# Latent attention with two 64-row tiles in the TensorE array

## The chip, the cores and the metric

The kernel runs on one core of a Trainium2 chip. A core has TensorE (matrix products, into PSUM), VectorE, ScalarE and GpSimd (element by element), and SyncE, whose queue here issues nearly all transfers. A matmul holds a stationary operand of up to 128 rows and 128 columns, loaded ahead of it, and streams a moving operand of up to 512 columns through it. The metric is the device time of one execution in microseconds; less is better. The time of the kernel before is the median of three runs.

## The reference

Two layers over 1024 latent tokens and 256 context tokens, width 1024: a windowed attention, then a multi-head latent attention; at the end a normalisation. The change is in the second layer's attention. It has 16 heads. Queries and keys have 64 dimensions without position ("nope") and 32 with rotary position ("rope"); the rope keys are shared by all heads. Only latent tokens are queries, 1280 tokens are keys:

```python
q  = (rms_norm(cq, q_norm) @ w_uq).reshape(b, n, 16, 64 + 32)
kv = (rms_norm(ckv, kv_norm) @ w_ukv).reshape(b, n, 16, 64 + 64)
# kn, v: halves of kv; kr: one 32-wide rope key for all heads
s = (einsum("bqhd,bkhd->bhqk", qn, kn) + einsum("bqhd,bkd->bhqk", qr, kr)) * scale
p = softmax(s, axis=-1)
o = einsum("bhqk,bkhd->bqhd", p, v)
y = (o * silu(g)) @ w_out
```

## The kernel before

All products but a few are made in three matmuls of reduced-precision float32 operands: each operand is split into a high part and a remainder, and high x high, remainder x high and high x remainder are summed in PSUM (`mm3`, lines 125 to 127). `split` (lines 120 and 121) makes the parts: ScalarE casts, VectorE or GpSimd subtracts.

The latent attention runs over 32 units, one per head and half of the queries (512). Keys of a head lie as 100 rows by 1280 columns in one of three buffers: 64 nope rows, 32 rope rows and four rows of ones. Queries lie the same way, and their last four rows take the negative row maxima, so that the product already holds score minus maximum. A unit has these steps:

- `prep`: two loads from DRAM bring its queries.
- `top(b)`, for four blocks of 128 queries: three matmuls (line 1122; 512, 512 and 256 keys, high parts only) write the scores into PSUM banks 0 to 2, and VectorE reduces them to the negative maximum (line 1126).
- `shift`: TensorE transposes the maxima (line 1130), ScalarE writes them into the query rows in four pieces (line 1133).
- `score(c)`, for ten key blocks of 128: `mm3` into one of banks 3 to 5, ScalarE takes the exponential (line 1141), GpSimd adds it to a running sum (lines 1145 and 1148), for the denominators.
- `PV`: ten plain float32 matmuls (line 1156), each run by the chip as two, of 64 stationary columns; even key blocks go to output rows 0 to 63, odd ones to 64 to 127. `fin` adds the two halves (lines 1170, ScalarE, and 1171, VectorE).
- `fin2`: four transpositions (line 1181) of the running sum and a VectorE sum (line 1182). `fin3`, for every second head only, brings the reciprocals to the rows by four more (line 1199), multiplies (line 1200, then GpSimd) and stores.

Every fourth unit makes the next two heads' keys (`make_K`, three blocks, each 6 matmuls, split into the key buffers), and every eighth the values of four heads (`make_V`, 60 matmuls of 256 columns). The third product matrix `w_out` is loaded and split in 16 pieces meanwhile, and when the last unit runs, the output tiles (`out_tiles`) begin.

A loop at the end interleaves the steps: between the ten scores of a unit stand the maxima of the next, `fin2` and `fin3` of the one before and pieces of K, V and `w_out`. The tile framework then sets the order of each engine's instructions from its own priorities, so that a matmul can move ahead of one that stands before it in the source; each engine then runs its list strictly in order, and semaphores make it wait for operands and for buffers.

## Time and profile before

| | |
|---|---|
| median of 3 runs | 1681.49 us (1681.13 to 1683.01) |
| profiled execution, span | 1678.9 us |
| TensorE busy | 1594.1 us, 95% |
| VectorE, ScalarE, GpSimd busy | 996.2, 831.6, 808.4 us |
| first value product starts | 1060.0 us |
| value products 9 and 17 start | 1199.1 and 1335.6 us |
| matmuls of the maxima (line 1122) | 384 |
| reductions of the maxima (line 1126) | 128, 1488 ns each |
| exponentials (line 1141) | 320, 597 ns each |

Rows of the trace in order of time give the start, the duration (merged for neighbours of one kind, with their count behind the x), the engine, the line, the operation, the output and input, their shapes and, in brackets, how long the engine was idle before it and what ended that. PE is TensorE's matmuls, PEld its weight loads, DVE VectorE, ACT ScalarE, POOL GpSimd, SPq the queue on SyncE. A matmul's duration runs to its result and so overlaps with its successor; what a matmul costs is read from start to start. In the rows by stretch stand the stretch, its length, busy time and count of PE, PEld, DVE, ACT and POOL, the granted clock, the transfer share and GB/s.

### The profile page before, as it was taken

The page shows a single profiled execution, that of the slowest core. Times are in us where ns is not written, and L with a number is a line of the kernel's source. Part 1 is how long each engine was busy: PE and PEld are TensorE (multiplying, and loading weights), DVE is VectorE, ACT ScalarE, POOL GpSimd, SP SyncE. Part 2 cuts the span into 40 slices and gives each one's busy share as a digit, 9 for nine tenths or more (in the row PEclk, how much of TensorE's full clock was granted, in tenths as well). Part 3 has the DMA queues.
Part 4 walks back from the last instruction along what each step waited for, and adds up shares of the span by engine and source line. Part 5 has one row for each costly group of instructions (what it writes and reads, how often), then busy time and mean ns, then how long its engine had stood idle before and what let it go on. Part 6 is the DMA issues. An engine that isn't in the chain of part 4 may idle for free.

```text
span 1678.9 us, 24936 instructions
## 1 busy us (share of the span) xinstructions
PE 1594.1 (95%) x8724; PEld 1247.4 (74%) x8724; DVE 996.2 (59%) x2004; ACT 831.6 (50%) x1790; POOL 808.4 (48%) x780
## 2 busy tenths in 40 slices
...
PEclk9999869999999999999999999999999999999999
...
GB/s 309 139 170 164 149 176 163 50 151 161 119 104 101 95 89 89 89 53 229 39 49 229 231 89 58 110 50 24 61 32 32 54 20 54 33 88 70 46 157 63
DMA packets 134206, 175.78 MB, mean 105 GB/s; under 512 B 11184, under 2 KB 79408, under 8 KB 134080
## 3 DMA queue, kind: packets, MB, share of 16 engines
...
HBM read 127.99 MB, written 46.15 MB: 104 GB/s over the span
## 4 chain that ended last, share of the span: by engine, by line
PE 72%; DVE 11%; ACT 6%; issue 5%; POOL 4%; DMA 2%; SPq 0%; DVEq 0%; POOLq 0%; ACTq 0%
PE PB L125 15%; PE PB L127 15%; PE PB L126 15%; PE PB L1156 9%; PE PB L1122 4%; PE PB L583 3%; PE PB L573 3%; DVE arena_r L121 2%; DVE arena_f L194 2%; PE PB L545 2%; DVE arena_f L552 1%; POOL arena_f L446 1%; PE PB L546 1%; DMA arena_f<-ada_w 1%; DVE arena_f L275 1%
## 5 line engine op out<-in xcount | busy, mean ns | idle before, releaser
L125 PE MATMUL PB<-arena_r 128*128 128x512 f32 (+3 forms) x1816 | 639.5, 353 | 20.3 <-DVE arena_f L445 13.4
L126 PE MATMUL PB<-arena_r 128*128 128x512 f32 (+3 forms) x1816 | 630.7, 348 | 3.6 <-DVE arena_r L280 2.6
L127 PE MATMUL PB<-arena_r 128*128 128x512 f32 (+3 forms) x1816 | 627.8, 347 | 0.6 <-DVE arena_r L121 0.6
L125 PEld LDWEIGHTS PB<-arena_r 128*128 128x128 f32 (+1 forms) x1816 | 346.2, 191 | 97.3 <-issue 26.0
L127 PEld LDWEIGHTS PB<-arena_r 128*128 128x128 f32 (+1 forms) x1816 | 345.5, 191 | 42.5 <-DVE arena_r L121 1.2
L126 PEld LDWEIGHTS PB<-arena_r 128*128 128x128 f32 (+1 forms) x1816 | 346.7, 191 | 40.5 <-DVE arena_r L280 4.5
L1148 POOL TENSOR_TENSOR arena_f<-arena_f 128x512 f32<-128x512 f32 x252 | 326.0, 1294 | 76.9 <-ACT arena_f L1141 61.9
L1141 ACT ACTIVATE arena_f<-PB 128x512 f32<-128x512 f32 x320 | 188.8, 597 | 124.5 <-PE PB L127 110.5
L1126 DVE TENSOR_REDUCE arena_f<-PB 128x1 f32<-128x1280 f32 x128 | 190.4, 1488 | 96.5 <-PE PB L1122 94.1
L121 DVE TENSOR_TENSOR arena_r<-PB,arena_r 128x512 fp32r<-128x512 f32 (+4 forms) x255 | 162.5, 644 | 139.7 <-ACT arena_r L120 138.2
L121 POOL TENSOR_TENSOR arena_r<-arena_f,arena_r 128x512 fp32r<-128x512 f32 x98 | 139.4, 1437 | 182.9 <-ACT arena_r L120 139.8
L120 ACT CAST arena_r<-PB 128x512 fp32r<-128x512 f32 (+4 forms) x255 | 137.8, 549 | 68.7 <-PE PB L573 29.7
L552 DVE CUSTOM_DVE_ANT_0 arena_f<-PB,arena_f,small 128x256 f32<-128x256 f32 (+1 forms) x288 | 145.7, 523 | 28.0 <-PE PB L546 21.8
L1156 PE MATMUL PB<-arena_f 128*64 128x512 f32 x640 | 156.0, 599 | 0.0
L194 DVE SCALAR_TENSOR_TENSOR arena_f<-arena_f,small 128x512 f32<-128x512 f32 x126 | 125.8, 1042 | 22.2 <-DMA arena_f<-ada_w 22.0
L555 ACT ACTIVATE arena_f<-arena_f,small 128x640 f32<-128x640 f32 (+2 forms) x160 | 119.4, 747 | 28.4 <-DVE small L554 27.1
L120 ACT CAST arena_r<-arena_f 128x512 fp32r<-128x512 f32 (+2 forms) x146 | 86.7, 609 | 86.6 <-DVE arena_f L455 18.6
L583 PE MATMUL PB<-arena_r 128*128 128x512 f32 x336 | 123.2, 440 | 4.4 <-ACT arena_f L594 3.2
L573 PE MATMUL PB<-ident,arena_f 128*128 128x128 f32 x672 | 110.5, 274 | 1.1 <-ACT arena_f L555 1.0
L1156 PEld LDWEIGHTS PB<-arena_f 128*64 128x64 f32 x640 | 43.4, 136 | 80.4 <-issue 79.2
L1122 PE MATMUL PB<-arena_r 96*128 96x512 f32 (+1 forms) x384 | 100.3, 369 | 1.0 <-DVE arena_f L1126 0.9
L573 PEld LDWEIGHTS PB<-ident,arena_f 128*128 128x128 f32 x672 | 83.4, 140 | 19.4 <-ACT arena_f L555 5.0
...
## 6 DMA issues: line engine op xcount, KB each, us to landing
arena_f<-ada_w SPq DMA_DIRECT2D x82, 256.0 KB, 3.3
arena_r<-q_d SPq DMA_DIRECT2D x80, 256.0 KB, 4.0
arena_f<-a_w_in SPq DMA_DIRECT2D x40, 256.0 KB, 3.0
...
g_d<-arena_f SPq DMA_DIRECT2D x36, 256.0 KB, 3.2
...
arena_r<-qn_d SPq DMA_DIRECT2D x32, 256.0 KB, 3.5
```

The source lines that it names most:

```text
L120: nc.scalar.copy(hi, src)
L121: (lo_eng or nc.vector).tensor_sub(lo, src, hi.bitcast(F32))
L125: nc.tensor.matmul(o, ah, bh, start=first, stop=False)
L126: nc.tensor.matmul(o, al, bh, start=False, stop=False)
L127: nc.tensor.matmul(o, ah, bl, start=False, stop=last)
L573: nc.tensor.transpose(pt[:, h, :], self.Ps[h][:, ci * 128 : ci * 128 + 128], ident)
L583: nc.tensor.matmul(self.pv, V[:, self.chunks[ci], self.g, :], PT[:, s], start=ci == 0 and s == 0, stop=ci == self.m - 1 and s == 1,)
L1122: nc.tensor.matmul(psm[:, n0 : n0 + n], self.qT[0:96, 0, b * 128 : b * 128 + 128], kt[0:96, 0, n0 : n0 + n], start=True, stop=True,)
L1126: nc.vector.reduce_max(self.mx[:, 96 + b : 97 + b], psm[:, 0:TOK], AX.X, negate=True)
L1141: nc.scalar.activation(E, S, AF.Exp)
L1148: eng.tensor_add(self.acc, self.acc, E)
L1156: nc.tensor.matmul(self.pv[p : p + 64], Vq[:, c, self.h % 4, :], self.E.pop(c), start=c < 2, stop=c >= NT - 2)
```

## The change

Scores and maxima are taken with 64 stationary rows instead of 100. The upper and the lower 64 rows of the array form two tiles; matmuls on them use different rows and write different PSUM banks.

- **Keys.** A head's nope keys lie twice 64 rows by 768 columns: rows 0 to 63 hold key blocks 0 to 3, rows 64 to 127 blocks 4 to 7, and both hold blocks 8 and 9. There are four such buffers. The rope keys, the same for all heads, are made once: `kr1` has high part and remainder in 64 rows, `kr2` the high part and four rows of ones.
- **Queries.** They lie on both tiles, so `prep` issues eight loads instead of two. `shift` writes the maxima by two VectorE multiplies instead of four ScalarE ones.
- **Scores.** Key blocks go in pairs, one on each tile, in five passes (three for nope, two for rope): ten matmuls instead of six for two blocks. One exponential takes 1024 columns.
- **Maxima.** Two matmuls of 512 keys on each tile and two of 256 on one of them, six instead of three.
- **PSUM.** Scores, shift, `fin2`, `fin3`, K and V share two slots of two banks (banks 3 to 6) in turn; the value product has bank 7.
- **Order.** The value product of a unit stands behind the first two scores of the next, with `fin`, the shift, `fin3` and `fin2` behind it. TensorE runs in source order from the first unit on; the other engines' orders are still made by the framework.
- **w_out** is staged in one buffer instead of three.

On TensorE, around the value product of a unit without K or `fin3`, before (a row of L125 to L127 is a score's matmul, L1122 a maximum, L1130 the shift's transposition, L1156 the value product):

```order
L125 MATMUL PB<-arena_r 128x512
L1130 MATMUL PB<-ident,arena_f 100x128
L126 MATMUL PB<-arena_r 128x512
L127 MATMUL PB<-arena_r 128x512
L1122 MATMUL PB<-arena_r 128x512 x2
L1122 MATMUL PB<-arena_r 128x256
L1156 MATMUL PB<-arena_f 64x512 x10
L125 MATMUL PB<-arena_r 128x512
```

And now (L1144 and L1147 are a maximum, L1175 scores, L1197 the value product, L1154 the shift, L1222 `fin2`):

```order
L1175 MATMUL PB<-arena_r 128x512 x16
L1144 MATMUL PB<-arena_r 128x512 x4
L1147 MATMUL PB<-arena_r 128x256 x2
L1197 MATMUL PB<-arena_f 64x512 x10
L1154 MATMUL PB<-ident,arena_f 100x128
L1222 MATMUL PB<-ident,arena_f 128x128 x4
L1144 MATMUL PB<-arena_r 128x512 x4
L1147 MATMUL PB<-arena_r 128x256 x2
L1175 MATMUL PB<-arena_r 128x512 x16
```

The shift's transposition has moved from ahead of the value product to behind it, `fin2` from the middle of the scores to the same place.

On VectorE at the same place, before (L1171 `fin`'s add, L1126 a maximum, L1182 `fin2`'s sum):

```order
L1171 TENSOR_TENSOR arena_f<-PB,arena_f 64x512
L1126 TENSOR_REDUCE arena_f<-PB 128x1
L1182 TENSOR_REDUCE small<-PB 128x4
L1126 TENSOR_REDUCE arena_f<-PB 128x1 x3
L1171 TENSOR_TENSOR arena_f<-PB,arena_f 64x512
```

And now (L1156 the shift's multiplies, L1212 `fin`'s add, L1223 `fin2`'s sum, L1149 a maximum, L1151 the copy of the maxima):

```order
L1149 TENSOR_REDUCE arena_f<-PB 128x1 x3
L1151 COPY arena_f<-arena_f 128x4
L1156 TENSOR_TENSOR arena_r<-PB,ident 4x512
L1212 TENSOR_TENSOR arena_f<-PB,arena_f 64x512
L1156 TENSOR_TENSOR arena_r<-PB,ident 4x512
L1223 TENSOR_REDUCE small<-PB 128x4
L1149 TENSOR_REDUCE arena_f<-PB 128x1 x4
```

Four instructions now stand between the fourth maximum of one unit and the first of the next; before, one stood between two maxima.

On TensorE where K is made, now, with the semaphores that an instruction waits for (L1237 is `fin3`, L125 to L127 K's product):

```order
L1197 MATMUL PB<-arena_f 64x512 x10
L1154 MATMUL PB<-ident,arena_f 100x128 [waits DVE_49,Activation_49]
L1237 MATMUL PB<-ident,arena_f 128x128 [waits Activation_49]
L1237 MATMUL PB<-ident,arena_f 128x128 x3
L1222 MATMUL PB<-ident,arena_f 128x128 [waits Pool_49]
L1222 MATMUL PB<-ident,arena_f 128x128 x3
L125 MATMUL PB<-arena_r 128x512 [waits DVE_49]
```

K's first matmul now waits for VectorE, which has to be done with the slot's last user.

The diff, cut:

```diff
--- before
+++ after
...
+    PAIRS = ((0, 4), (1, 5), (2, 6), (3, 7), (8, 9))
...
-    kTb = [r_at(o, 2, TOK) for o in (0, 16, 26)]
-    qtr = Ring(R, [10, 36, 40], 1024)
-    Er = Ring(F, [10 + 2 * c for c in range(NT)], 512)
-    accr = Ring(F, [30, 32], 512)
+    kTb = [r_at(6 * i, 2, 768) for i in range(4)]
+    kr1, kr2 = r_at(24, 768), r_at(27, 768)
+    qtb = [[r_at(o, 2, 512), r_at(o1, 512), r_at(o2, 512)] for o, o1, o2 in ((30, 34, 36), (38, 42, 112), (104, 108, 110))]
+    qt0 = [[r_at(o, 2, 512), r_at(o + 4, 512), r_at(o + 6, 512)] for o in (80, 88)]
+    Er = Ring(F, [10 + 4 * i for i in range(6)], 1024)
...
+    psm = PB[:, 0:3, :]
+    slots = Banks((3, 2), (5, 2))
+    pv_bank = PB[:, 7, :]
...
+    def slot():
+        return shp(slots(), 2, 512)
...
+    def make_kr():
...
+            w = slice(512 * (n // 2), 512 * (n // 2) + 128 * cn)
+            for t in (0, 1) if n == 2 else (n,):
+                p = 64 * t
+                src = pt[0:32, 0 : cn * 128]
+                split(kr1[p : p + 32, w], kr1[p + 32 : p + 64, w], src)
+                nc.scalar.copy(kr2[p : p + 32, w], src)
+        for p in (32, 96):
+            nc.gpsimd.tensor_copy(kr2[p : p + 4], const[p : p + 4, 0:1].to_broadcast([4, 768]))
...
+    def make_K(pair, blocks):
+        sl = slot()
+        for j, blk in enumerate(blocks):
+            n0, n = ((0, 512), (512, 512), (1024, 256))[blk]
+            ps = sl[:, j]
...
+        for j, blk in enumerate(blocks):
+            w = slice(0, 512) if blk < 2 else slice(512, 768)
             for e in range(2):
-                kt = kTb[(2 * pair + e) % 3]
-                split(kt[0:64, 0, n0 : n0 + n], kt[0:64, 1, n0 : n0 + n], ps[64 * e : 64 * e + 64, 0:n])
...
+                kt = kTb[(2 * pair + e) % 4]
+                for t in (0, 1) if blk == 2 else (blk,):
+                    p = 64 * t
+                    split(kt[p : p + 64, 0, w], kt[p : p + 64, 1, w], sl[64 * e : 64 * e + 64, j, 0 : w.stop - w.start])
...
         def prep(self):
-            q = shp(qtr.next(), 2, 512)
+            self.q = n, r1, r2 = qt0[self.i] if self.i < 2 else qtb[self.i % 3]
             ts = slice(self.half * 512, self.half * 512 + 512)
             e, r = 64 * self.e, 32 * (self.h % 4)
-            load(out=q[0:64].bitcast(F32), in_=qn_d[self.pair, e : e + 64, :, ts])
-            load(out=q[64:96].bitcast(F32), in_=qr_d[self.h // 4, r : r + 32, :, ts])
-            self.qT = q
+            for t in range(2):
+                load(out=n[64 * t : 64 * t + 64].bitcast(F32), in_=qn_d[self.pair, e : e + 64, :, ts])
+            for t in range(4):
+                load(out=r1[32 * t : 32 * t + 32].bitcast(F32), in_=qr_d[self.h // 4, r : r + 32, 0, ts])
+            for t in range(2):
+                load(out=r2[64 * t : 64 * t + 32].bitcast(F32), in_=qr_d[self.h // 4, r : r + 32, 1, ts])
             self.mx = mxr.next()
 
         def top(self, b):
-            kt = kTb[self.h % 3]
-            for n0, n in KEYB:
-                nc.tensor.matmul(
-                    psm[:, n0 : n0 + n], self.qT[0:96, 0, b * 128 : b * 128 + 128], kt[0:96, 0, n0 : n0 + n],
-                    start=True, stop=True,
+            n, r1, _ = self.q
+            bs = slice(b * 128, b * 128 + 128)
+            pairs = ((n[:, 0, bs], self.kt[:, 0]), (r1[:, bs], kr1))
+            rs = [slice(64 * t, 64 * t + 64) for t in range(2)]
+            for i, (q, k) in enumerate(pairs):
+                for t in range(2):
+                    nc.tensor.matmul(psm[:, t], q[rs[t]], k[rs[t], 0:512], start=i == 0, stop=i == 1)
+            for i, (q, k) in enumerate(pairs):
+                r = rs[b % 2]
+                nc.tensor.matmul(psm[:, 2, 0:256], q[r], k[r, 512:768], start=i == 0, stop=i == 1)
+            flat = psm.rearrange("p a b -> p (a b)")[:, 0:TOK]
+            nc.vector.reduce_max(self.mx[:, 32 + b : 33 + b], flat, AX.X, negate=True)
+            if b == 3:
+                nc.vector.tensor_copy(self.mx[:, 96:100], self.mx[:, 32:36])
+
+        def shift(self, pm):
+            nc.tensor.transpose(pm[0:100, 0:128], self.mx[:, 0:100], ident)
+            for p in (32, 96):
+                nc.vector.tensor_mul(
+                    shp(self.q[2][p : p + 4], 4, 128),
+                    pm[p : p + 4, 0:128].unsqueeze(1).to_broadcast([4, 4, 128]),
+                    ident[p : p + 4, p : p + 4].unsqueeze(2).to_broadcast([4, 4, 128]),
                 )
-            nc.vector.reduce_max(self.mx[:, 96 + b : 97 + b], psm[:, 0:TOK], AX.X, negate=True)
-
-        def shift(self):
-            pm = psx()[:, 0:128]
-            nc.tensor.transpose(pm[0:100], self.mx[:, 0:100], ident)
-            for b in range(4):
-                o = self.qT[96:100, 0, b * 128 : b * 128 + 128]
-                nc.scalar.activation(o, pm[96:100], AF.Copy, scale=ident[96:100, 96 + b : 97 + b])
-
-        def score(self, c):
-            kt = kTb[self.h % 3]
-            S = pst4()
-            cs = slice(c * 128, c * 128 + 128)
-            mm3(S, [kt[0:100, s, cs] for s in range(2)], [self.qT[0:100, s] for s in range(2)], True, True)
-            E = Er.next()
-            nc.scalar.activation(E, S, AF.Exp)
-            self.E[c] = E
-            if c == 1:
+
+        def score(self, i, a=0, b=5, hold=False):
+            n, r1, r2 = self.q
+            kt = self.kt
+            if a == 0:
+                self.S = slot()
+            S = self.S
+            c0 = (i * 128, i * 128) if i < 4 else (512, 640)
+            passes = [(kt[:, 0], n[:, 0], 64), (kt[:, 1], n[:, 0], 64), (kt[:, 0], n[:, 1], 64)]
+            passes += [(kr1, r1, 64), (kr2, r2, 36)]
+            for j in range(a, b):
+                k, q, rows = passes[j]
+                for t in range(2):
+                    r = slice(64 * t, 64 * t + rows)
+                    nc.tensor.matmul(S[:, t], k[r, c0[t] : c0[t] + 128], q[r], start=j == 0, stop=j == 4)
+            if b == 5 and not hold:
+                self.expo(i)
+
+        def expo(self, i):
+            E = shp(Er.next(), 2, 512)
+            nc.scalar.activation(E, self.S, AF.Exp)
+            self.E[i] = E
+            if i == 0:
                 self.acc = accr.next()
-                nc.gpsimd.tensor_add(self.acc, self.E[0], E)
-            elif c:
-                eng = nc.vector if self.i == NU - 1 and c > 5 else nc.gpsimd
-                eng.tensor_add(self.acc, self.acc, E)
+                nc.gpsimd.tensor_add(self.acc, E[:, 0], E[:, 1])
+                return
+            for t in range(2):
+                eng = nc.vector if self.i == NU - 1 and i > 2 else nc.gpsimd
+                eng.tensor_add(self.acc, self.acc, E[:, t])
 
         def PV(self):
-
-
-            self.pv = psv()
-            for c in range(NT):
-                p = 64 * (c % 2)
-                nc.tensor.matmul(
-                    self.pv[p : p + 64], Vq[:, c, self.h % 4, :], self.E.pop(c), start=c < 2, stop=c >= NT - 2
-                )
+            self.pv = pv_bank
+            for i, cs in enumerate(PAIRS):
+                E = self.E.pop(i)
+                for t in range(2):
+                    p = 64 * t
+                    nc.tensor.matmul(
+                        self.pv[p : p + 64], Vq[:, cs[t], self.h % 4, :], E[:, t], start=i == 0, stop=i == 4
+                    )
...
+        st = f_at(45, 512)
+        pieces = [(k, slice(c * 512, c * 512 + 512)) for k in (0, 1, 2, 3, 4, 6, 7, 5) for c in range(2)]
+        for i in range(len(pieces) + 1):
+            if i:
+                k, cs = pieces[i - 1]
+                split(WoB[k][:, 0, cs], WoB[k][:, 1, cs], st)
...
                 k, cs = pieces[i]
-                st = ring.next()
                 load(out=st, in_=t["b_w_out"][k * 128 : k * 128 + 128, cs])
...
-                yield
+            yield
...
+    with tc.manual_schedule(engines={mybir.EngineType.PE}):
+        u1.top(0)
+        u0.shift(slot()[:, 0])
+        u1.top(1)
+        for ui, u in enumerate(units):
+            pu, ppu = [units[ui - n] if ui >= n else None for n in (1, 2)]
+            nu, nnu = [units[ui + n] if ui + n < NU else None for n in (1, 2)]
+            if nnu:
                 nnu.prep()
-            u.score(c)
-            if nnu and c == 9:
+            u.score(0, 0, 2)
+            if nu:
+                nu.top(2)
+            u.score(0, 2, 5)
+            u.score(1, hold=True)
+            if nu:
+                nu.top(3)
+            if ui % 2 and 5 <= ui < 24 or 25 <= ui:
+                next(wo_fill, None)
+            if ui == NU - 1:
+                next(wo_fill, None)
+                next(out_fill)
+            if pu:
+                pu.PV()
+                u.expo(1)
+                pu.fin()
+                sl = slot()
+                if nu:
+                    nu.shift(sl[:, 0])
+                if ppu and ppu.e == 1:
+                    ppu.fin3(slot()[:, 0])
+                pu.fin2(sl[:, 1])
+            else:
+                u.expo(1)
+                nu.shift(slot()[:, 0])
+            if ui % 4 == 0 and u.pair < 7:
+                make_K(u.pair + 1, (0, 2))
+            if ui % 4 == 1 and u.pair < 7:
+                make_K(u.pair + 1, (1,))
+            if ui and ui % 8 == 0:
+                for _ in make_V(u.pair // 2):
+                    pass
+            if ui == NU - 1:
+                next(out_fill)
+            if nnu:
                 nnu.top(0)
-            if c == 9:
...
+            u.score(2)
+            u.score(3, 0, 3)
+            if nnu:
+                nnu.top(1)
+            u.score(3, 3, 5)
+            u.score(4)
...
```

`hold` keeps the exponential of the second score back until the value product stands in the lists; `fin`, `fin2` and `fin3` take the slot that they are handed and are otherwise as before.

156 lines of the change are left out of this document (49 added, 107 removed).

## The prediction

> **What bounds the kernel now.** I read the page's engine totals first, then the busy time of stretches cut at the starts of value products eight units apart.
>
> ```profile
> PE 1594.1 (95%) x8724; PEld 1247.4 (74%) x8724; DVE 996.2 (59%) x2004; ACT 831.6 (50%) x1790; POOL 808.4 (48%) x780
> PEclk9999869999999999999999999999999999999999
> 1199.10:1335.60 136.50, 136.17 (x651) 88.87 (x650) 69.18 (x69) 73.14 (x147) 97.42 (x76) 1.00 0.13 41
> 1335.60:1472.00 136.40, 136.07 (x649) 88.87 (x648) 69.50 (x69) 72.75 (x147) 97.05 (x76) 1.00 0.12 39
> ```
>
> In the latent-attention stage TensorE sets the time: eight units take 136.5 us, TensorE is busy for 136.2 of them at full clock (1.00), and VectorE (69) and ScalarE (73) have half their time free. One unit costs 136.5 / 8 = 17.06 us. The order of time on TensorE shows what that consists of:
>
> ```profile
> 1199.13 4.51 PE L1156 MATMUL PB<-arena_f 128*64 128x512 f32 x20
> 1203.57 0.50 PE L125 MATMUL PB<-arena_r 100*128 100x512 f32 x1
> 1203.91 0.39 PE L126 MATMUL PB<-arena_r 100*128 100x512 f32 x1
> 1204.13 0.40 PE L127 MATMUL PB<-arena_r 100*128 100x512 f32 x1
> 1204.37 0.75 PE L1122 MATMUL PB<-arena_r 96*128 96x512 f32 x3
> 1204.95 0.39 PE L125 MATMUL PB<-arena_r 100*128 100x512 f32 x1
> 1207.03 0.60 PE L1181 MATMUL PB<-ident,arena_f 128*128 128x128 f32 x4
> 1207.39 0.84 PE L1122 MATMUL PB<-arena_r 96*128 96x512 f32 x3
> 1208.06 0.39 PE L125 MATMUL PB<-arena_r 100*128 100x512 f32 x1
> ...
> 1212.93 0.75 PE L1122 MATMUL PB<-arena_r 96*128 96x512 f32 x3
> 1213.61 4.51 PE L1156 MATMUL PB<-arena_f 128*64 128x512 f32 x20
> ```
>
> Durations overlap, so I count from start to start. A score matmul steps 0.23 (1203.91 to 1204.13). A maximum (three matmuls of 512, 512, 256 keys) takes 0.58 (1204.37 to 1204.95), so 0.23 + 0.23 + 0.12. The value product takes 4.44 to the next matmul (1199.13 to 1203.57), and that one's successor comes 0.34 later, not 0.23. Four transpositions take 1208.06 - 1207.03 - 0.58 = 0.45. A unit without extras is 30 x 0.23 + 4 x 0.58 + 4.44 + 0.45 + about 0.3 = 14.4. Eight of them, two K products (each 12 steps of 0.23 and 6 of 0.12: 3.5), one V product (60 x 0.12 = 7.2) and four `fin3` (0.45 each) make 131; so about 5 us in 136.5 are waits.
>
> **What the change removes and adds on TensorE.** Scores: 25 pairs of matmuls instead of 30 matmuls. The price of a pair is not in the trace. The nearest rows are weight loads of the value product, whose two 64-column halves already lie side by side:
>
> ```profile
> 1214.09 0.14 PEld L1156 LDWEIGHTS PB<-arena_f 128*64 128x64 f32 x2 [0.29 <-issue]
> 1214.52 0.14 PEld L1156 LDWEIGHTS PB<-arena_f 128*64 128x64 f32 x2 [0.28 <-issue]
> 1204.84 0.19 PEld L125 LDWEIGHTS PB<-arena_r 100*128 100x128 f32 x1
> 1204.96 0.19 PEld L126 LDWEIGHTS PB<-arena_r 100*128 100x128 f32 x1
> ```
>
> Two loads share one 0.14, and twenty matmuls fit into 10 steps of 0.43 (4.3 of the 4.44): the halves run at the same time. Bounds for a pair: 0.23 (wholly side by side), 0.38 (two loads of 0.19 in series), 0.46 (two matmuls in series). I take 0.235: the value product is the nearest row, and two 128-column loads were started 0.12 apart, so even serial loads nearly fit. Scores: 25 x 0.235 = 5.9 instead of 6.9, a gain of 1.0. A maximum becomes two pairs and two matmuls of 256 on one tile, 2 x 0.235 + 2 x 0.12 = 0.71; four of them 2.84 instead of 2.32, a loss of 0.5. The switch into the value product's column tiles costs 0.1 (1212.93 to 1213.61 is 0.68, not 0.58), the way out another 0.1 (4.44 against 4.3) and 0.11 for the weight load behind it (0.34 against 0.23). A unit now has three modes (rows, columns, whole array) instead of two: 0.2 more. A plain unit's matmuls come to 14.1, 0.3 less than now. So TensorE has little to win; without any wait a mean unit would be 14.1 + 0.22 (`fin3`) + 0.87 (K) + 0.9 (V) = 16.1.
>
> **The waits that come in.** TensorE is now in source order, with nothing of another unit to slip in. The rows that price what it waits for:
>
> ```profile
> 1218.05 0.50 PE L125 MATMUL PB<-arena_r 100*128 100x512 f32 x1
> 1218.19 0.58 ACT L1170 COPY arena_f<-PB 64x512 f32<-64x512 f32 x1 [3.45 <-PE PB L1156]
> 1218.86 0.68 DVE L1171 TENSOR_TENSOR arena_f<-PB,arena_f 64x512 f32<-64x512 f32 x1 [3.66 <-ACT arena_f L1170]
> 1207.67 0.69 DVE L1182 TENSOR_REDUCE small<-PB 128x4 f32<-128x512 f32 x1 [1.02 <-PE PB L1181]
> 1208.28 1.48 DVE L1126 TENSOR_REDUCE arena_f<-PB 128x1 f32<-128x1280 f32 x1
> 1209.91 0.75 PE L1122 MATMUL PB<-arena_r 96*128 96x512 f32 x3
> L1141 ACT ACTIVATE arena_f<-PB 128x512 f32<-128x512 f32 x320 | 188.8, 597 | 124.5 <-PE PB L127 110.5
> ```
>
> Let N be the start of the first matmul behind the value product (1218.05 in these rows). In the new VectorE order four things stand between the value product and the next unit's first maximum: a shift multiply, `fin`'s add, a second shift multiply, `fin2`'s sum. The multiply (4x512 from PSUM) is new; bounds 0.42 (a 64x256 operand, shown below) and 0.69 (64x512); I take 0.69, since 512 columns go through in either. The shift transposition ends at N + 0.4; multiply to 1.1; the add could start at N + 0.81 (1218.86) and so follows at once, to 1.8; second multiply to 2.5; sum to 3.2; then the reduction of maximum 0, 1.49, to 4.7. TensorE: shift and `fin2` to N + 0.65, mode 0.85, maximum 0 to 1.55, score 2 to 2.75. Score 3 needs the two-bank slot that shift and `fin2` used: it waits for the sum, until 3.35 (0.6 lost), and runs its first three passes to 4.05. Maximum 1 needs the maxima's banks back: 4.7 + 0.15 (the rows above: 1208.28 + 1.48 to 1209.91) = 4.85 (0.8 lost), to 5.55. Rest of score 3, score 4: 7.2. The next unit's score 0 takes score 3's slot, whose exponential (1024 wide: 0.60 for 512 and 0.21 per 256 more, about 1.03) began at 6.3, ended at 7.35, so start at 7.5 (0.3 lost). Scores 0 and 1 and maxima 2 and 3 take 3.78, the value product 4.54 with its entry: next N at 15.8. **14.1 of work and 1.7 of waits.**
>
> The K units come off worse. Their rows, and those of the loads:
>
> ```profile
> 1221.71 0.58 ACT L120 CAST arena_r<-PB 64x512 fp32r<-64x512 f32 x1 [0.73 <-PE PB L127]
> 1432.58 0.37 ACT L120 CAST arena_r<-PB 64x256 fp32r<-64x256 f32 x1
> 1432.98 0.42 DVE L121 TENSOR_TENSOR arena_r<-PB,arena_r 64x256 fp32r<-64x256 f32 x1 [1.61 <-ACT arena_r L120]
> 1213.12 0.52 SPq L1114 DMA_DIRECT2D arena_r<-qn_d  x1
> arena_r<-qn_d SPq DMA_DIRECT2D x32, 256.0 KB, 3.5
> arena_f<-b_w_out SPq DMA_DIRECT2D x16, 256.0 KB, 3.0
> ```
>
> With `fin3` in front, TensorE reaches K at N + 1.1, but K's slot is the shift's: it waits for the second multiply, to 2.65 (1.5 lost). The 512 block ends at 4.05, when the sum (3.9 with `fin3`'s multiply) has just freed the other bank; the 256 block ends at 4.75; maximum 0 and score 2 end at 6.85. Score 3 then needs K's slot back: two casts of 0.58, four of 0.37 and two reciprocal copies on ScalarE from 4.3 on, with subtractions and a 1.49 reduction between them on VectorE, to about 9.5 (some 3 lost before its second tile). With 0.45 + 2.08 more work the unit is about 21.5. The unit after it makes the third K block (1.4): 1.5 lost ahead of it, 1.8 behind, about 19.6. Every eighth unit V adds 7.2 but hides most of K's second wait: 4.3 net.
>
> Eight units: 2 x (15.8 + 16.0 + 21.5 + 19.6) + 4.3 = 150, against 136.5: **+13.6**. Units 4 to 27 are three such groups: +41. For the first four and last four I take the plain excess: 15.8 against (136.5 - 7.0 - 7.2 - 1.8) / 8 = 15.1, so +5. Sum +46; the profiled span of 1678.9 becomes 1725, and since the median of the runs, 1681.49 (1681.13 to 1683.01), lies 2.6 above that span, the time is **1727**.
>
> Edits at nothing: eight loads per unit instead of two take 8 x 0.55 = 4.4 of SP's queue; the sixth, the last that maximum 0 needs, is issued 3.3 and lands 3.5 later, at 6.8 of a unit whose maximum 0 comes at 9.5. If that cover goes, maximum 0 and all behind it wait. ScalarE loses the four shift products and VectorE gets them. GpSimd's nine additions stay (97 us busy in 136.5). The stage ahead of the attention and the output tiles behind it change only their buffers.
>
> The Trainium skill, TensorEngine Tiling (Array Packing), Performance Considerations (PSUM Bottleneck), says that tiling speeds up the array but not the emptying of PSUM, which may become the bottleneck; by that rule the change hits its wall in VectorE's 1.48 reductions, as the sum above has it. The row agrees so far: a reduction takes 1.48 and its matmuls 0.58.
>
> **Rivals.**
>
> *The waits stay covered (faster).* If the VectorE burst behind the value product ended by N + 1.8, when maximum 0's banks are full, instead of 3.2, maximum 1 would wait for nothing, and score 3 neither; with K's splits hidden too, only the 16.1 of work are left: 1.0 less than now, 32 x 1.0 = 32, **1649**. For it: VectorE is half idle. Against it: the order of its instructions is fixed, each of the four has a row near 0.69, and at 0.42 per multiply the burst still ends at 2.65; the unit would be about 15.3, and the total 1711.
>
> *A pair costs more than a matmul (slower).* Halfway, 0.30: 33 pairs a unit x 0.065 = 2.1, of which the waits for VectorE take up about 0.8: +1.3 x 32 = 42, **1769**. At 0.38: about 1830; at 0.46: 33 x 0.225 = 7.4, less 1.6: 1910. For it: no row here has 64-row tiles. Against it: the shared 0.14 load. The Trainium skill, TensorE: Matmul & The Clock Gate, Part 3 (Measured speedup against the span model), has four 32-row tiles at 3.07 times, not 4; carried over to two tiles that is an estimate of 0.30 per pair, the first of these cases. No run here shows it yet.
>
> *Loads come into the way (slower).*
>
> ```profile
> 1200.05 0.62 ACT L120 CAST arena_r<-arena_f 128x512 fp32r<-128x512 f32 x1
> 1200.70 0.81 DVE L121 TENSOR_TENSOR arena_r<-arena_f,arena_r 128x512 fp32r<-128x512 f32 x1
> ```
>
> `w_out` now has one staging buffer: cast 0.62, subtraction 0.81, issue 0.52, landing 3.0, so 5 us per piece, and nine pieces stand in ScalarE's queue between the exponentials of the first three units, their loads ahead of unit 5's on SP. Nine x 5 = 45 us against about 45 of units. If they or the eight loads cost 1 us a unit: **1760**.
>
> *Gains and waits cancel:* 1681.
>
> **Chances.** Forecast 0.62; covered waits 0.17; dearer pair 0.09; loads 0.08; no change 0.04. Faster by over 0.2% 0.17, within 0.2% (about what repeated timings tell from nothing) 0.04, slower 0.79. Range 1668 to 1775: below it lies most of the covered case, above it the far end of the dear pair and of the loads; the forecast alone is 1705 to 1750 (multiplies at 0.42, or pairs at 0.25).
>
> **What would show it.** Score pairs starting 0.23 to 0.24 apart, the two of a pair within 0.02; on TensorE, idle time ahead of the maxima and of score 3 released by VectorE, about 1.7 us per plain unit, 4.5 in the K units; value products 15.8 apart in plain units, 150 per eight. TensorE's busy share in the stage falls from 0.99 to about 0.9. Wrong if the maxima's reduction starts right behind its matmuls, if waits name DMA, or if the pairs start 0.3 or more apart.

## The result, and the profile after

| | before | after |
|---|---|---|
| median of the runs | 1682.25 us (1681.13 to 1685.54) | 1766.32 us (1763.58 to 1770.75) |
| profiled span | 1678.9 us | 1764.2 us |
| value products 1, 9, 17, 25, 32 start | 1060.0, 1199.1, 1335.6, 1472.0, 1589.0 | 1083.3, 1239.0, 1392.1, 1546.5, 1670.0 |

The change makes the kernel 1.0502 times as long (95% interval 1.0483 to 1.0521): 84 us slower, where 46 were forecast. The page of the kernel after, its engine totals and the granted clock in 40 slices:

```profile
PE 1609.3 (91%) x9738; PEld 1256.0 (71%) x9738; DVE 1074.4 (61%) x2111; ACT 775.5 (44%) x1509; POOL 799.7 (45%) x772
PEclk9999969999999999999999998989999999998999
```

TensorE's share falls from 95% to 91%, and the clock row, flat before from the seventh slice on, has eights in it. The stage by stretches, from value product 1 to 9, 17, 25 and 32 (columns as in the prediction), and behind it the last of these for the kernel before:

```profile
1083.34:1239.03 155.69, 139.34 (x901) 91.26 (x900) 94.18 (x103) 62.61 (x83) 96.48 (x76) 0.96 0.23 64
1239.03:1392.11 153.08, 138.25 (x906) 90.44 (x905) 88.80 (x96) 58.33 (x75) 96.86 (x77) 0.97 0.24 63
1392.11:1546.52 154.41, 137.07 (x906) 87.32 (x905) 93.44 (x99) 59.61 (x78) 98.18 (x77) 0.99 0.26 68
1546.52:1670.03 123.51, 112.92 (x681) 70.32 (x680) 65.27 (x69) 44.12 (x52) 82.69 (x65) 0.93 0.25 71
```

```profile
1472.03:1589.01 116.98, 116.53 (x529) 74.86 (x528) 55.27 (x55) 58.41 (x117) 82.85 (x64) 1.00 0.19 61
```

Eight units take 153.1 to 155.7 instead of 136.5 (139.1 for the first eight), with TensorE idle for 15 to 17 of them and the clock below 1.00. Stretch by stretch the excess is 23.3 ahead of the first value product, 16.6, 16.6, 18.0, then 6.5 in the last seven units and 4.3 behind them: 85.3, the difference of the two spans. A plain unit, TensorE and then VectorE in order of time:

```profile
1275.18 4.51 PE L1197 MATMUL PB<-arena_f 128*64 128x512 f32 x20
1279.63 0.32 PE L1154 MATMUL PB<-ident,arena_f 128*100 128x128 f32 x1
1279.78 0.60 PE L1222 MATMUL PB<-ident,arena_f 128*128 128x128 f32 x4
1280.31 0.73 PE L1144 MATMUL PB<-arena_r 64*128 64x512 f32 x4
1280.88 0.28 PE L1147 MATMUL PB<-arena_r 64*128 64x256 f32 x1
1280.88 0.39 PE L1175 MATMUL PB<-arena_r 64*128 64x512 f32 x1
1280.99 0.28 PE L1147 MATMUL PB<-arena_r 64*128 64x256 f32 x1
...
1282.86 0.97 PE L1175 MATMUL PB<-arena_r 64*128 64x512 f32 x5 [0.18 <-DVE small L1223]
1284.26 0.73 PE L1144 MATMUL PB<-arena_r 64*128 64x512 f32 x4 [0.43 <-DVE arena_f L1149]
...
1288.15 2.01 PE L1175 MATMUL PB<-arena_r 64*128 64x512 f32 x15
1289.90 0.73 PE L1144 MATMUL PB<-arena_r 64*128 64x512 f32 x4
...
1290.80 0.65 PE L1197 MATMUL PB<-arena_f 128*64 128x512 f32 x2
```

```profile
1279.98 0.68 DVE L1156 TENSOR_TENSOR arena_r<-PB,ident 4x512 fp32r<-4x512 f32 x1 [1.97 <-PE PB L1154]
1280.68 0.69 DVE L1212 TENSOR_TENSOR arena_f<-PB,arena_f 64x512 f32<-64x512 f32 x1
1281.39 0.70 DVE L1156 TENSOR_TENSOR arena_r<-PB,ident 4x512 fp32r<-4x512 f32 x1
1282.11 0.69 DVE L1223 TENSOR_REDUCE small<-PB 128x4 f32<-128x512 f32 x1
1282.72 1.48 DVE L1149 TENSOR_REDUCE arena_f<-PB 128x1 f32<-128x1280 f32 x1
```

The unit takes 15.62, from one value product to the next (forecast 15.8). N is again the start of the first matmul behind the value product, 1279.63. VectorE's burst is what the prediction drew: two multiplies, the add and the sum at 0.7 each, then the reduction; score 3 waits for the sum, and maximum 1 starts at 1284.26, N + 4.63 (forecast N + 4.85). The brackets show only 0.18 and 0.43 because a matmul's 0.39 runs on past its successor's start; from start to start the trace has 0.57 and 0.82 there, and 0.43 ahead of the next unit's score 0, instead of 0.23, with 0.11 more behind each: 1.5 in all (forecast 1.7). The fifteen score matmuls from 1288.15 to 1289.90, 7.5 pairs in 1.75, give 0.233 a pair: two tiles do run side by side at the price of one matmul. The K units, TensorE:

```profile
1297.75 0.50 PE L125 MATMUL PB<-arena_r 128*128 128x512 f32 x1 [1.32 <-DVE arena_r L1156]
...
1303.54 0.50 PE L1175 MATMUL PB<-arena_r 64*128 64x512 f32 x1 [1.37 <-DVE arena_r L121]
1305.70 0.97 PE L1175 MATMUL PB<-arena_r 64*128 64x512 f32 x5 [1.67 <-DVE arena_r L121]
```

Here the waits are those of the prediction too (1.5 ahead of K, 3 ahead of score 3). What it did not have is in the clock (the column behind POOL's) of these two K units and, in the last row, of the 3.4 us from 1306.80 on, behind the last of the waits above. The third row is another second K unit:

```profile
1290.80:1313.96 23.16, 18.79 (x116) 13.00 (x115) 13.69 (x17) 8.85 (x14) 13.26 (x12) 0.93 0.25 65
1313.96:1334.49 20.53, 17.62 (x110) 11.48 (x110) 11.25 (x12) 6.87 (x8) 12.77 (x11) 0.92 0.27 71
1392.11:1411.54 19.43, 16.54 (x110) 10.35 (x109) 11.53 (x12) 6.87 (x8) 13.61 (x11) 1.00 0.25 71
1306.80:1310.20 3.40, 3.40 (x21) 2.90 (x19) 1.49 (x1) 1.02 (x1) 0.67 (x1) 0.56 0.00 0
```

The two second K units wait alike (1.31 and 1.60 in that from 1313.96, 1.31 and 1.57 in that from 1392.11), but only in the earlier one does the clock fall, and it takes 1.1 longer.

### The profile page after: what moved, and what is told of

Same layout as the page of the kernel before. It is cut to its first block, busy times and chain, and to the rows that moved or that the text cites. A ratio compares the mean times of both kernels' runs of the same rounds, so it can differ in the third digit from the quotient of the medians.

```text
span 1764.2 us, 26875 instructions
## 1 busy us (share of the span) xinstructions
PE 1609.3 (91%) x9738; PEld 1256.0 (71%) x9738; DVE 1074.4 (61%) x2111; ACT 775.5 (44%) x1509; POOL 799.7 (45%) x772
## 3 DMA queue, kind: packets, MB, share of 16 engines
q10 hardware_dynamic: 1760, 2.56, 0.5%
## 4 chain that ended last, share of the span: by engine, by line
PE 59%; DVE 17%; ACT 8%; POOL 6%; issue 5%; DMA 3%; SPq 0%; ACTq 0%; POOLq 0%; DVEq 0%
PE PB L125 10%; PE PB L127 10%; PE PB L126 10%; PE PB L1175 7%; PE PB L1197 6%; DVE arena_r L121 3%; PE PB L583 3%; PE PB L1144 3%; PE PB L573 3%; POOL arena_f L1189 2%; DVE arena_f L1149 2%; DVE arena_r L1156 2%; DVE arena_f L194 2%; ACT arena_r L120 2%; PE PB L545 2%
## 5 line engine op out<-in xcount | busy, mean ns | idle before, releaser
L125 PE MATMUL PB<-arena_r 128*128 128x512 f32 (+2 forms) x1496 | 508.8, 341 | 38.5 <-DVE arena_r L1156 15.8
L126 PE MATMUL PB<-arena_r 128*128 128x512 f32 (+2 forms) x1496 | 504.6, 337 | 3.9 <-DVE arena_r L280 2.6
L127 PE MATMUL PB<-arena_r 128*128 128x512 f32 (+2 forms) x1496 | 502.3, 336 | 0.5 <-DVE arena_r L121 0.5
L125 PEld LDWEIGHTS PB<-arena_r 128*128 128x128 f32 x1496 | 285.7, 191 | 75.1 <-DVE arena_r L1156 18.6
L126 PEld LDWEIGHTS PB<-arena_r 128*128 128x128 f32 x1496 | 286.1, 191 | 33.4 <-DVE arena_r L280 4.5
L127 PEld LDWEIGHTS PB<-arena_r 128*128 128x128 f32 x1496 | 285.7, 191 | 29.4 <-DVE arena_r L121 1.1
L1175 PE MATMUL PB<-arena_r 64*128 64x512 f32 (+1 forms) x1600 | 263.4, 426 | 35.7 <-DVE arena_r L121 23.9
L1149 DVE TENSOR_REDUCE arena_f<-PB 128x1 f32<-128x1280 f32 x128 | 190.6, 1489 | 137.1 <-PE PB L1147 136.7
L1175 PEld LDWEIGHTS PB<-arena_r 64*128 64x128 f32 (+1 forms) x1600 | 188.2, 201 | 87.1 <-DVE arena_r L121 29.9
L1181 ACT ACTIVATE arena_f<-PB 128x1024 f32<-128x1024 f32 x160 | 163.7, 1026 | 195.5 <-PE PB L1175 133.1
L121 DVE TENSOR_TENSOR arena_r<-PB,arena_r 128x512 fp32r<-128x512 f32 (+3 forms) x266 | 166.1, 631 | 136.8 <-ACT arena_r L120 135.4
L120 ACT CAST arena_r<-PB 128x512 fp32r<-128x512 f32 (+3 forms) x266 | 141.2, 539 | 110.9 <-PE PB L127 54.1
L1197 PE MATMUL PB<-arena_f 128*64 128x512 f32 x640 | 144.4, 597 | 0.0
L120 ACT CAST arena_r<-arena_f 128x512 fp32r<-128x512 f32 (+2 forms) x146 | 87.2, 609 | 116.6 <-DMA arena_f<-b_w_out 22.6
L1144 PE MATMUL PB<-arena_r 64*128 64x512 f32 x512 | 97.5, 436 | 10.8 <-DVE arena_f L1149 10.7
```

The costliest lines, as they stand in the source:

```text
L120: nc.scalar.copy(hi, src)
L121: (lo_eng or nc.vector).tensor_sub(lo, src, hi.bitcast(F32))
L125: nc.tensor.matmul(o, ah, bh, start=first, stop=False)
L126: nc.tensor.matmul(o, al, bh, start=False, stop=False)
L127: nc.tensor.matmul(o, ah, bl, start=False, stop=last)
L1149: nc.vector.reduce_max(self.mx[:, 32 + b : 33 + b], flat, AX.X, negate=True)
```

## The experiments

Four causes stood against one another: VectorE's burst and the buffers (the prediction's), the clock, the start with the `w_out` loads, and the source order of TensorE or the tiles themselves. Times are medians; the kernel before took 1682.2 to 1683.3 beside them.

### Loads in source order

```diff
-    with tc.manual_schedule(engines={mybir.EngineType.PE}):
+    with tc.manual_schedule(engines={mybir.EngineType.PE, mybir.EngineType.SP}):
```

> The changed kernel with one thing altered: the loads keep the order of the source too (as TensorE does), so that the pieces of w_out come when the units 5, 7, 9 and so on ask for them, and not in the queue of the first three units. Nothing else is left out. My theory after the result: of the 23.3 us that the first value product comes later (1060.0 before, 1083.3 now), about 6 are work moved ahead of it, and some 15 come from the w_out casts that stand in ScalarE's queue of the first units and wait for their loads (waits of 2 to 3 us each on the row of the cast from b_w_out). By it the first value product starts at 1066 to 1072, ScalarE's waits for b_w_out go, the rest of the stage keeps its 153 us per eight units, and the time is 1745 to 1757. The rival: VectorE's maxima and the low clock set the start, and ScalarE waits beside them; then the first value product stays at 1080 to 1084 and the time at 1761 to 1770.

Measured: 1758.7. The theory fell at its place: the first value product starts at 1086.2, not earlier. The waits of ScalarE for the loads did go down, in the list of waits of the kernel after and of this one (sum, times, longest):

```profile
ACT arena_r L120 <- DMA arena_f<-b_w_out: 22.6, 10, 3.0
```

```profile
ACT arena_r L120 <- DMA arena_f<-b_w_out: 9.5, 12, 1.8
```

The 7.6 us (4.5 between the two profiled executions) came from elsewhere: the second and third value products follow after 17.8 and 15.7 instead of 20.5 and 17.4, the last unit with V takes 26.4 instead of 29.5, and the later start takes 2.9 of it back. So the order of the loads costs 7.6, and the start is something else. The edit puts all loads of SyncE's queue into source order, not those of `w_out` alone; that it was the casts which held these units up is argued from the two rows of waits.

### The shift's multiplies later

```diff
-            nc.tensor.transpose(pm[0:100, 0:128], self.mx[:, 0:100], ident)
+            nc.tensor.transpose(shift_ps[0:100], self.mx[:, 0:100], ident)
+
+        def shift2(self):
...
             if nnu:
                 nnu.top(0)
+            if nu:
+                nu.shift2()
```

`shift_ps` is `PB[:, 2, 256:384]`, and `shift2` the two multiplies. VectorE keeps the source order too.

> The changed kernel with the shift's two multiplies taken out of the VectorE burst behind the value product: the shift's transposition goes into the unused half of the third maxima bank, and the multiplies stand behind the next unit's first maximum. VectorE keeps the order of the source, so that only the add of fin and the sum of fin2 (2 x 0.69 instead of 4) stand ahead of the first maximum. My theory (the burst sets the waits of a plain unit): the first maximum ends 0.8 to 1.4 earlier, value products of plain units stand 14.7 to 15.0 apart instead of 15.6, K's first matmul no longer waits 1.3 for the multiplies, and eight units take 141 to 147 instead of 153; with what VectorE's source order changes at the start, 1715 to 1745 in all. The rival (pairs or transfers set the pace, and VectorE's waits only lie beside that): plain units stay at 15.6 and the time at 1760 to 1770.

Measured: 1767.2, plain units 15.5. The first reduction does move ahead, and K no longer waits; but the multiplies now read the third maxima bank, and the next maximum has to wait for them there. TensorE and VectorE (L1148 a maximum, L1159 the multiplies in this kernel):

```profile
1265.84 0.38 PE L1148 MATMUL PB<-arena_r 64*128 64x256 f32 x1 [0.69 <-DVE arena_r L1159]
```

```profile
1264.39 1.39 DVE L1159 TENSOR_TENSOR arena_r<-PB,ident 4x512 fp32r<-4x512 f32 x2
```

The burst was not shortened, only turned round: the same 1.4 of multiplies stands ahead of the second maximum instead of the first. This neither proves nor refutes the theory; it shows that in this program the wait goes by the whole bank: the matmul writes columns 0 to 255 and still waits for a read of columns 256 to 383.

### Work in the waits

```diff
+            if ui % 4 < 2 and u.pair < 7:
+                filler(psm[:, 0], 5)
             if ui % 4 == 0 and u.pair < 7:
                 make_K(u.pair + 1, (0, 2))
...
             u.score(2)
+            if ui % 4 < 2 and u.pair < 7:
+                filler(pv_bank, 11 if ui % 4 == 0 else 5)
```

> The changed kernel with more work: in the two units of every four that make K, TensorE multiplies something that nobody reads while it would wait: five matmuls of 512 columns ahead of K's product and eleven (five in the second of the two units) ahead of score 3, some 28 us of matmuls in all that fit into waits of 1.3, 3.0 and 1.6 us. It tells whether the falls of the granted clock come from the waits. If they do (my theory now): the stretches at half clock go from the K units, the granted clock of the eight units from 1083 to 1239 and from 1239 to 1392 rises from 0.96 and 0.97 to 1.00, eight units take 148 to 150 instead of 153 to 155.7, and the time falls to 1745 to 1758 although TensorE has more to do. The rival (the clock falls for another reason, or its fall costs nothing because the waits cover it): the clock stays at 0.96 to 0.97 and the time at 1764 to 1775.

Measured: 1765.5, no gain, though the clock of the stretches rose to 1.00 (the filler is 182 matmuls, so some 42 us and not the 28 of the expectation). The K units did gain, 19.4 instead of mostly 20.5 and 22.1 instead of 23.2 to 24.0; the units that make V as well lost it again (29.3 instead of 26.4), since V already fills their wait and eleven matmuls came on top. So once more without those:

```diff
-                filler(pv_bank, 11 if ui % 4 == 0 else 5)
+                filler(pv_bank, 0 if ui % 8 == 0 and ui else 11 if ui % 4 == 0 else 5)
```

> The filler matmuls again, without those ahead of score 3 in the three units that make V: the run with the filler had 19.4 instead of 20.5 in the second K units and 22.1 instead of 23.2 to 24 in the first, but 29.3 instead of 26.4 in the V units, where the filler met no wait. My theory (the fall of the granted clock to a half costs 1.1 to 1.9 in each K unit): second K units 19.4, first 22.1, V units 26.4 or a little less, eight units near 150, which is what the prediction had, and 1750 to 1757 in all. The rival (the V units' excess was no misplaced filler, but heat or a budget that the chip takes back): V units stay at 28 to 29.3 and the time at 1762 to 1768.

Measured: 1757.1, with 26.4 in two of the three V units (29.5 in the last, as in the kernel after). The two K units, and the eight units from the ninth value product on:

```profile
1288.48:1310.58 22.10, 21.56 (x133) 14.17 (x132) 13.70 (x17) 8.86 (x14) 12.76 (x11) 1.00 0.23 67
1310.58:1330.00 19.42, 19.02 (x120) 12.05 (x119) 11.88 (x12) 6.88 (x8) 12.78 (x11) 1.00 0.27 76
```

```profile
1237.81:1387.64 149.83, 144.95 (x946) 93.50 (x945) 90.58 (x96) 58.34 (x75) 97.03 (x77) 1.00 0.23 64
```

TensorE has more to do (21.6 busy instead of 18.8 in the first K unit) and is done sooner. The waits are not shorter, only filled; what they cost beyond their own length was the clock, 9.2 us in all. At full clock these eight units take 149.8; the prediction had 150.

### The passes of a tile one after the other

```diff
-            for j in range(a, b):
-                k, q, rows = passes[j]
-                for t in range(2):
+            for t in range(2):
+                for j in range(a, b):
+                    k, q, rows = passes[j]
```

> The changed kernel with the two loops inside a score exchanged: all passes of the upper tile, then all passes of the lower one, so that two neighbours in the list use the same 64 rows and can't run side by side except at the seam. Same work, same waits asked for. My theory (a pair costs 0.229 because its two matmuls run at the same time): a score takes 10 x 0.23 = 2.3 less one overlap of 0.23 instead of 1.15, so 5 x 0.9 = 4.6 more per unit, of which the waits for VectorE take up at most 1.5; 32 x 3.1 to 4.6 = 100 to 150 more, 1865 to 1915. The rival (the pair is fed in turn, and order within a score matters little): within 20 of 1766.

Measured: 1771.9, 5.5 more than the change, and 16.0 instead of 15.6 for a plain unit. The theory fell as far as the order goes. Score 2 and three passes of score 3, sixteen matmuls, now listed five, five, three and three by tile:

```profile
1264.11 2.68 PE L1175 MATMUL PB<-arena_r 64*128 64x512 f32 x16
1267.23 0.73 PE L1144 MATMUL PB<-arena_r 64*128 64x512 f32 x4 [0.44 <-DVE arena_f L1149]
```

One after the other, sixteen would need 16 x 0.23 = 3.7; they take 2.68, and side by side eight pairs would take some 1.9. In the trace the lower tile's first matmul starts 0.24 behind the upper tile's first, beside its second, with three of the upper tile's still to come: matmuls of the other tile overtake. So this run did not take the overlap away, and the saving by tiles is not measured by it.

### TensorE's order left to the framework

```diff
-    with tc.manual_schedule(engines={mybir.EngineType.PE}):
+    if True:
```

> The changed kernel without the source order of TensorE: the framework orders TensorE's instructions as it does those of the other engines; tiles, buffers and steps are those of the change. In the list that comes of it K's products stand behind the next maximum and score 2 instead of ahead of them, and the first maxima of the attention have some V and gate products between them; plain units keep the same order. My theory (the waits come from what VectorE does ahead of the next maximum and from buffers, not from the source order as such): plain units stay at 15.6, the K units lose their wait of 1.3 ahead of K and fall by 1 to 2 each, the first value product starts some 5 earlier, and the time is 1735 to 1760. The rival (source order on TensorE is what costs): plain units too come near the 15.1 of the kernel before, eight units near 140, and the time is 1690 to 1720.

Measured: 1752.2. Plain units stay at 15.6, so source order is not what costs there. Second K units fall from 20.5 to 18.2, since a maximum and a score stand ahead of K; but the wait is partly only moved, from K to score 3:

```profile
1319.03 0.50 PE L125 MATMUL PB<-arena_r 128*128 128x512 f32 x1 [0.42 <-DVE arena_r L1156]
...
1323.81 0.50 PE L1175 MATMUL PB<-arena_r 64*128 64x512 f32 x1 [1.07 <-DVE arena_r L121]
```

First K units stay at 23.1 to 24.3, against the expectation, and the start gains nothing: one matmul of the first value product moves up to 1069.6, its others do not, and the ninth starts at 1239.5 (1239.0 after). Its gain is uneven: 148.0 against 153.1 from the ninth value product to the seventeenth, 152.9 against 154.4 from there to the twenty-fifth, 3 in the last units, nothing in the first eight. By the second K units, K's place is most of it; the run does not part it from the clock, which is 0.98 to 0.99 here instead of 0.96 to 0.99.

### The start mixed with other products

The four maxima of unit 0, its shift and the first two maxima of unit 1 stand ahead of V and the gate products, and the source order begins only at the loop:

```diff
     u0, u1 = units[0:2]
-    u0.top(0)
-    next(vk)
-    u0.top(1)
+    for b in range(4):
+        u0.top(b)
+    u1.top(0)
+    u0.shift(slot()[:, 0])
+    u1.top(1)
     next(vk)
-    u0.top(2)
+    next(vk)
     g_tile(9, 4)
-    u0.top(3)
```

> The changed kernel with another order at the start of the attention alone: the four maxima of unit 0, its shift and the first two maxima of unit 1 stand ahead of the last V and gate products in the source, and the source order of TensorE begins only with the unit loop, so that the framework puts some fourteen products between two maxima. My theory (the first value product comes 23.3 later because, in source order, six maxima follow one another with nothing between them but a VectorE reduction each, 1.6 to 3.2 idle per maximum between 1049 and 1065, with the clock down behind it): the idle time there goes, the first value product starts at 1066 to 1075 instead of 1083, the units behind keep their times, and the time is 1750 to 1759. The rival (the w_out casts that wait in ScalarE's queue set the start): the first value product stays at 1080 to 1085.

Measured: 1757.4, the first value product at 1075.4. The start of the kernel after, maxima with a reduction of 1.48 each and nothing between them; and the one wait that is left of these in this run:

```profile
1051.40 0.73 PE L1144 MATMUL PB<-arena_r 64*128 64x512 f32 x4 [1.58 <-DVE arena_f L1149]
1053.95 0.74 PE L1144 MATMUL PB<-arena_r 64*128 64x512 f32 x4 [1.34 <-DVE arena_f L1149]
1056.90 1.22 PE L1144 MATMUL PB<-arena_r 64*128 64x512 f32 x4 [0.96 <-DVE arena_f L1149]
1065.15 0.42 PE L1154 MATMUL PB<-ident,arena_f 128*100 128x128 f32 x1 [2.91 <-DVE arena_f L1151]
```

```profile
1059.40 0.29 PE L1154 MATMUL PB<-ident,arena_f 128*100 128x128 f32 x1 [2.14 <-DVE arena_f L1151]
```

So the order of the start costs 8 to 9 of its 23.3.

### The three together

> The changed kernel with three of the alterations of the earlier runs at once: the start mixed with the V and gate products, the loads in source order, and the filler matmuls in the K units' waits. VectorE's burst behind the value product and the waits of a unit are left as they are. Alone they gave 1757.4, 1758.7 and 1757.1, that is 8.9, 7.6 and 9.2 less than 1766.3. If the three causes are separate, they add up: 1738 to 1744, with eight units at 150, and what then remains over the kernel before is the burst (13.5 per eight units, some 47) and some 10 at the start and the end. If they are one cause in three guises (the low clock, say), the sum is 1748 to 1756.

Measured: 1744.1, ratio 1.0366 (1.0344 to 1.0389); the sum of the three alone would be 1740.6. So 22.2 of the 25.7 add up: the causes are separate for the most part, though the time is at the edge of what was expected of that. The stretches:

```profile
1077.29:1226.31 149.02, 144.32 (x942) 93.20 (x941) 92.75 (x97) 59.55 (x77) 95.44 (x76) 1.00 0.22 59
1226.31:1376.19 149.88, 145.05 (x946) 93.46 (x946) 94.49 (x100) 60.73 (x79) 98.53 (x77) 1.00 0.25 71
1376.19:1526.81 150.62, 144.97 (x946) 93.49 (x945) 95.46 (x100) 60.77 (x79) 98.46 (x77) 1.00 0.26 71
```

What remains, 61 us over the kernel before (62.6 by the spans), is the burst together with the waits of the K units (9.9, 13.4 and 14.2 in the three groups, 3.6 in the last units), 17.3 at the start, where "some 10 at the start and the end" were expected, and 4.2 at the end.

### VectorE's work spread out

If the burst is the cause, it must go away with it. The loop of this version, cut; the start is the mixed one, and VectorE keeps the source order too:

```python
            if pu:
                pu.PV()
            u.expo(1)
            if pu:
                pu.fin()
            if ppu and ppu.e == 1:
                ppu.fin3(slot()[:, 0])
            if nnu:
                nnu.top(0)
...
            u.score(2)
            if nu:
                nu.shift(pv_bank[:, 0:128])
            if pu:
                pu.fin2(pv_bank[:, 128:132])
            if nu:
                nu.shift2()
            if pu:
                pu.fin2b()
            u.score(3)
            if nnu:
                nnu.top(1)
            u.score(4)
            if ui % 4 != 2 and kp < 8:
                K_mm(kp, kb, pv_bank)
```

`fin2` is four matmuls with a column of ones here, `fin2b` the copy of their 128x4 sums, `K_mm` the product of one block of K, which is split in the next unit.

> A version that should beat both, by the theory: the two tiles, scores and maxima as in the change, the start as in the run before this, and VectorE's work behind the value product spread out. The shift and fin2 go into the value product's own bank behind the second score, fin2 sums with a column of ones (four matmuls of one column, a copy of four numbers) instead of four transpositions and a reduction of 512 columns, the shift's multiplies stand behind the first maximum, and K is made one block per unit in the value product's bank behind the last score, split beside the next unit's scores. VectorE too keeps the source order. Only fin's add stands ahead of the first maximum. My theory (TensorE has 14.1 to 14.3 of work in a plain unit, the rest is waits for VectorE and buffers): plain units 14.2 to 14.7, eight units 130 to 137 with K and V, the clock at 1.00, first value product at 1066 to 1075, and 1660 to 1695 in all. The rival (four reductions of 1.48 with their matmuls of 0.71 set a pace of their own, or two tiles side by side draw the clock down): plain units above 15.2, the clock below 0.98, and 1720 or more.

Measured: 1721.6 (1.0244, 1.0219 to 1.0270), above the 1660 to 1695 of the theory. Plain units came to 14.7, upper end of the theory and without a wait on TensorE, so the burst, with the buffers that it holds, is the cause of their waits. Eight units took 144 to 146, not 130 to 137: the value product now waits until K's block has been split out of its bank:

```profile
1283.69 4.51 PE L1206 MATMUL PB<-arena_f 128*64 128x512 f32 x20 [1.09 <-DVE arena_r L121]
1301.98 1.51 PE L1206 MATMUL PB<-arena_f 128*64 128x512 f32 x6 [2.06 <-DVE arena_r L121]
```

```diff
+            if ui % 4 != 2 and kp < 8:
+                K_mm(kp, kb, pv_bank)
+                K_split(kp, kb, pv_bank)
             u.score(4)
-            if ui % 4 != 2 and kp < 8:
-                K_mm(kp, kb, pv_bank)
```

> The spread version again, with what its trace showed mended: K's block of a unit is made ahead of the last score instead of behind it and split at once, so that the value product no longer waits 1.2 to 2.3 for the split; the first unit has a score between two maxima that followed one another; and ScalarE too keeps the source order, so that no cast of the output stage waits for its load in the middle of the last units (3.6 in the run before). By the theory that waits of this kind are all that is left: 144 per eight units less 2 x 4.9 = 134 to 136 (136.5 in the kernel before), the last four units 67 to 70 instead of 71.8, 1676 to 1694 in all. The rival (ScalarE in source order brings waits of its own, exponentials held behind casts and copies): 1700 or more.

Measured: 1696.7 (1.0078, 1.0057 to 1.0100), eight units 138.1 to 138.6, both a little above what was expected. One wait was left in the stage, for an exponential behind four casts:

```profile
1223.03 1.43 PE L1184 MATMUL PB<-arena_r 64*128 64x512 f32 x10 [1.06 <-ACT arena_f L1190]
```

In the last unit TensorE waited 1.64 and 1.68 for the split of the first output tile and 2.81 for the copies of `fin3`'s reciprocals; ScalarE in source order brought waits of its own there, as the rival had it, though not 1700 in all: 71.2 for the last four units. Then (this is the edit on K)

```diff
-            for t in (0, 1) if blk == 2 else (blk,):
-                p = 64 * t
-                split(kt[p : p + 64, 0, w], kt[p : p + 64, 1, w], ps[64 * e : 64 * e + 64, 0 : w.stop - w.start])
+            p = 64 * (blk % 2)
+            split(kt[p : p + 64, 0, w], kt[p : p + 64, 1, w], ps[64 * e : 64 * e + 64, 0 : w.stop - w.start])
+            if blk == 2:
+                load(out=kt[64:128, :, w].bitcast(F32), in_=kt[0:64, :, w].bitcast(F32))
```

> The spread version with the last waits that its trace shows taken out: the 256 keys that lie on both tiles are split once and copied to the other tile by a transfer (two casts and subtractions instead of four; 1.46 idle in one unit of four), and at the end the split of the first output tile stands ahead of the last value products (waits of 2.2, 2.2 and 3.2). By the theory the kernel is then bound by TensorE's own work, which with tiles, modes and K is no less than before: eight units 135 to 136 against 136.5 before, 1676 to 1690 in all, so that two tiles side by side come out about even with the kernel before and no better. The rival (the copies queue behind each other, and a unit waits for its keys): 1695 or more.

Measured: 1688.6 (1.0038, 1.0023 to 1.0053), eight units as expected. In this run the load of the final gain overwrites a block of exponentials of one unit (the last but one) before its value product has read it, and the value product waits 3.45 for that load. So the output of this version is wrong, and only its stage ahead of that is read here:

```profile
1070.25:1205.58 135.33, 135.33 (x933) 89.85 (x933) 78.84 (x92) 57.79 (x73) 96.27 (x76) 1.00 0.24 64
1205.58:1341.53 135.95, 135.95 (x937) 90.30 (x936) 81.21 (x96) 58.74 (x75) 97.95 (x77) 1.00 0.30 82
1341.53:1477.44 135.91, 135.91 (x937) 90.20 (x936) 81.24 (x96) 58.84 (x76) 97.94 (x77) 1.00 0.31 82
```

TensorE is busy for all of the stretch, at full clock: no wait is left, and eight units take 135.9 against 136.5 before. That need not be the least that two tiles allow. A plain unit takes 14.67, and its `fin2` (eight matmul instructions of one column, 1228.36 to 1229.24) takes 0.88 from start to start, where the four transpositions of the change take 0.53 (1279.78 to 1280.31 above): 0.35 more per unit, 2.8 per eight.

> The spread version once more, now with less work for TensorE: the shift's transposition, fin2's four matmuls and fin3 stand together right behind the value product again, in the slot that is free there, so that the array changes its mode once there and not twice (0.33 into and 0.18 out of whole-array mode per unit by the starts of the run before), but VectorE does the shift's multiplies, the copy of the sums and fin3's multiply first, then the first maximum, and fin's add only behind that. The load of the final gain, which in the run before came so early that it overwrote a block of exponentials still to be read, is back behind the last-but-one value product. By the theory (nothing but TensorE's own work is left): plain units 14.1 to 14.3, eight units 131 to 133, 1664 to 1680 in all, under both kernels. The rival (the burst is back, and the second maximum or score 3 waits for it): plain units 14.8 or more, 1685 or more.

Measured: 1719.3 (1.0209, 1.0195 to 1.0223). The expectation failed: plain units stay at 14.7, and in one unit of four `fin3` waits, with the clock down behind it (20.7 instead of 17.0 for that unit):

```profile
1272.92 1.11 PE L1254 MATMUL PB<-ident,arena_f 128*128 128x128 f32 x4 [2.46 <-ACT arena_f L1248]
```

Its place behind the next unit's `fin2` was a mistake of mine: both write the same two buffers of reciprocals, so in those units `fin3` multiplies by those of the other half of the queries, and has to wait for them; the output of this version is wrong too. A plain unit has no idle time on TensorE here either, and takes 14.65 instead of 14.67: one switch of modes less does not show in it. No version ran below the kernel before.

## Why the prediction was right in sign, and where its size was wrong

The time, 1766.3 where 1727 was forecast, lies inside the range of 1668 to 1775, but above the 1705 to 1750 that stood for the forecast alone. That end of the range was kept for dear pairs (1769) and for loads (1760), and neither made the difference: a pair costs 0.233, and the order of the loads 7.6 of the 84. The sign and the waits were foreseen; that the time still fell inside the range is in part luck.

**Waits of the plain units: right.** 15.62 against 15.8, with the releasers and the places named, and pairs 0.233 apart against 0.235. The spread version, which differs in a plain unit by VectorE's order, the buffers that go with it and the form of `fin2`, has 14.7 with no wait left, though its `fin2` costs 0.35 more: shown, not argued.

**K units: right in kind, at full clock nearly in size.** 22.1 and 19.4 against 21.5 and 19.6. Four plain units at 15.65, 22.1, 26.4 and two of 19.4 make 149.9; the prediction's "Eight units: ... = 150" is what the second filler run (149.8 from the ninth value product on) and the three together (149.0 to 150.6) measured.

**The clock: missed, 9 us.** "Eight units ... 150, against 136.5: +13.6" took every matmul at full clock. In most K units the same waits brought 3.4 us at half clock behind them, 16.6 to 18.0 per group instead of 13.6 (the last group has the late `w_out` casts in it as well). I had read 1.00 in every row of before and carried it over to a kernel that idles.

**Start and end: the step that failed.** "For the first four and last four I take the plain excess: ... so +5". The start alone is 23.3, the last units and the end 10.8. Of the start, 8 to 9 are the order of the first maxima, which in source order follow one another with only VectorE between. With the order mended 15.4 was left (1075.4 against 1060.0). Three more maxima, two scores of the next unit and K's first product now stand ahead of the first value product: some 3 x 0.71 + 2 x 1.15 + 2.1 less 1.0 for the cheaper scores, 5.5 of work. The trace of that run has three waits there, 2.14 (shown above), 1.16 and 1.68, with a stretch of 3.4 us at half clock (0.50) behind them, where the kernel before has one wait of 0.3: by these figures some 6.5 more. The other 3.5 were not taken apart, and the 10.8 of the last units and the end neither.

**Loads: nothing in the sum, 7.6 measured.** The eight loads were put at nothing, the loads of `w_out` only into a rival, at 1 us a unit. They cost less than the rival had, but not nothing: with 9.5 us of casts waiting in ScalarE's queue instead of 22.6 the kernel ends 7.6 earlier. What the single buffer costs by itself no run shows.

**Rivals.** Dearer pairs fell: 0.233. The estimate of 0.30 was worked out from the four tiles of 32 rows in the Trainium skill, TensorE: Matmul & The Clock Gate, Part 3 (Measured speedup vs the span model), and the trace doesn't bear it out for two tiles of 64 rows. Covered waits fell twice: they were not covered, and where a version covers them, eight units take 135.9 and not the 8 x 16.1 = 129 that I gave for TensorE's work without waits. That version is not the change without its waits: 2.8 of the 135.9 are its dearer `fin2`, it makes K in three pieces, and its output is wrong behind the stage. Without the 2.8 it would take some 133, an estimate from the two prices of `fin2`. So the 7.7 per eight units that the prediction had for covered waits were 0.5 in the one run without waits, some 3 by that estimate; how much more is to be had stays open.
